# The first store and the fourth load in one queue: combining two expert outputs per token

## The chip, the cores and the metric

The kernel runs on one core of a Trainium2 chip. The metric is the device time in microseconds (us), the median over several executions. The core has five engines with instruction queues of their own; this kernel computes on VectorE (DVE in the profile) and a little on ScalarE (ACT), and moves data with the core's 16 DMA engines. Transfers are issued from two queues: that of SyncE (SP in the profile, DMA queue q1) and that of ScalarE (DMA queue q10).

## The reference

For each of 16 x 1024 tokens there are two expert outputs of 512 floats and two weights; the result is their weighted sum.

```python
def setup_inputs():
    batch, seq, hidden, n_experts, k = 16, 1024, 512, 8, 2
    return {
        "expert_outputs": np.random.randn(batch, seq, k, hidden).astype(np.float32),
        "combine_weights": np.random.randn(batch, seq, k).astype(np.float32),
    }

def reference(expert_outputs, combine_weights):
    weights = combine_weights[..., np.newaxis]
    return np.sum(expert_outputs * weights, axis=2).astype(np.float32)
```

67.1 MB of expert outputs are read and 33.6 MB of results are written, all in 32-bit floats.

## The kernel before

The 16,384 tokens are laid over 128 partitions, 128 tokens in each. A token's column holds both expert outputs, 1024 floats (4 KB), so a column over all partitions is 512 KB to load and 256 KB to store. The 128 columns are cut into ten tiles of 13 or 12 columns (`TILES`). In SBUF there is one buffer `et` with four rooms (`ROOM`), in which the tiles go round: tile g lies in room g mod 4. Tile 0 is loaded in two pieces of 2 and 11 columns, so that there are eleven loads (L76, the helper `load`), all of them issued from SyncE's queue. The weights come in three small transfers from ScalarE's queue (L79 and L114), behind an 8 KB store of zeros into a part of the output that is written again later (L111).

The order is written out by hand (`manual_schedule`); waits follow from the data and from a small set of completion semaphores that the transfers share in turn. First come the loads of tiles 0 to 3, in four rooms (`FIRST`). Then a loop runs over the stores (`STORES`): a round combines its tile, issues the store of the result, and issues the load of the tile four further on. That load goes into the room that the store reads from, so it waits for the store to have landed.

How a tile is combined (`combine`): for tiles 0 to 7 VectorE multiplies the whole room in place by the broadcast weights (L88) and adds the two halves into the beginning of the room (L97). Tile 8 is shared between ScalarE (L92) and VectorE (L94, L96, L97). Tile 9 goes column by column, ScalarE scaling one half (L102) and VectorE doing the other and the addition in one instruction (L103). Tiles 7 and 8 are stored together, and tile 9's result goes to room 0.

Stores are issued at L130: rounds 0 to 6 from ScalarE's queue, the joint store of tiles 7 and 8 and that of tile 9 from SyncE's. So before the change SyncE's queue holds: the loads of tiles 0, 1, 2, 3, then 4 to 9, each behind its wait, then two stores. ScalarE's queue holds the zeros, the weights, seven stores, and ScalarE's computing for tiles 8 and 9.

Of the kernel before, what the change touches and what calls it, by code (L numbers as in the profile page):

```python
# [1 line left out]

# [4 lines left out]


@with_exitstack
def kernel(  # L10
    ctx: ExitStack,
    tc: tile.TileContext,
    expert_outputs: bass.AP,
    combine_weights: bass.AP,
    out: bass.AP,
):

    nc = tc.nc
    b, s, k, h = expert_outputs.shape
    assert k == 2
    n = b * s
    P = nc.NUM_PARTITIONS
    per = n // P
    assert per * P == n

    ROOM = [13, 13, 12, 13]
    ROOMS = len(ROOM)  # L30
    SITE = [sum(ROOM[:i]) for i in range(ROOMS)]
    TILES = [13, 13, 12, 13, 13, 13, 12, 13, 13, 13]
    FIRST = [2, 11, 13, 12, 13]
    STORES = [[0], [1], [2], [3], [4], [5], [6], [7, 8], [9]]
    WHOLE = [0, 1, 2, 3, 4, 5, 6, 7]
    MIXED = [8]
    ALONE = 3
    FREE = {9: 0}
    LAST = 13
    assert all(c <= ROOM[g % ROOMS] for g, c in enumerate(TILES))  # L40
    assert sum(TILES) == per and [g for st in STORES for g in st] == list(range(len(TILES)))
    main = per - LAST
    starts = [sum(TILES[:g]) for g in range(len(TILES))]

    def rows(x):

        first = x[0 : P * main, :].rearrange("(p t) f -> p t f", p=P)
        second = x[P * main : n, :].rearrange("(p t) f -> p t f", p=P)
        return lambda t, c: first[:, t : t + c, :] if t < main else second[:, t - main : t - main + c, :]

    flat = out.rearrange("b s h -> (b s) h")
    eo = rows(expert_outputs.rearrange("b s k h -> (b s) (k h)"))
    cw = rows(combine_weights.rearrange("b s k -> (b s) k"))
    o = rows(flat)

    dt = mybir.dt.float32
    mult = mybir.AluOpType.mult
    add = mybir.AluOpType.add
    copy = mybir.ActivationFunctionType.Copy

    pool = ctx.enter_context(tc.tile_pool(name="all", bufs=1))
    et = pool.tile([P, sum(ROOM), k * h], dt)
    halves = et.rearrange("p j (k h) -> p (j k) h", k=k)
    wt = pool.tile([P, per * k], dt)
    wk = wt.rearrange("p (t k) -> p t k", k=k)
    zt = pool.tile([16, 128], dt)
    warm = pool.tile([P, 1], dt)

    def place(t):
        g = max(g for g in range(len(TILES)) if starts[g] <= t)  # L70
        return SITE[g % ROOMS] + t - starts[g]

    def load(t, c, **kw):
        at = place(t)
        assert place(t + c - 1) == at + c - 1
        nc.sync.dma_start(out=et[:, at : at + c], in_=eo(t, c), **kw)  # L76

    def weights(q, t, c):
        q.dma_start(out=wk[:, t : t + c, :], in_=cw(t, c))  # L79

    def combine(g, base):
        at, c, t0 = SITE[g % ROOMS], TILES[g], starts[g]
        if g in WHOLE or g in MIXED:
            room = halves[:, k * at : k * (at + c), :]
            x0, x1 = et[:, at : at + c, 0:h], et[:, at : at + c, h : 2 * h]
            if g in WHOLE:
                wb = wt[:, k * t0 : k * (t0 + c)].unsqueeze(2).to_broadcast([P, k * c, h])
                nc.vector.tensor_tensor(out=room, in0=room, in1=wb, op=mult)  # L88
            else:
                for i in range(ALONE, c):  # L90
                    x = et[:, at + i, 0:h]
                    nc.scalar.activation(out=x, in_=x, func=copy, scale=wt[:, k * (t0 + i) : k * (t0 + i) + 1])  # L92
                w1 = wk[:, t0 : t0 + c, 1:2].to_broadcast([P, c, h])
                nc.vector.tensor_tensor(out=x1, in0=x1, in1=w1, op=mult)  # L94
                w0 = wk[:, t0 : t0 + ALONE, 0:1].to_broadcast([P, ALONE, h])
                nc.vector.tensor_tensor(out=x0[:, 0:ALONE], in0=x0[:, 0:ALONE], in1=w0, op=mult)  # L96
            nc.vector.tensor_tensor(out=halves[:, base : base + c, :], in0=x0, in1=x1, op=add)  # L97
            return
        for i in range(c):
            t = k * (t0 + i)  # L100
            x0, x1 = halves[:, k * (at + i), :], halves[:, k * (at + i) + 1, :]
            nc.scalar.activation(out=x0, in_=x0, func=copy, scale=wt[:, t : t + 1])  # L102
            nc.vector.scalar_tensor_tensor(  # L103
                out=halves[:, base + i, :], in0=x1, scalar=wt[:, t + 1 : t + 2], in1=x0, op0=mult, op1=add
            )

    with tc.manual_schedule():
        nc.vector.memset(zt, 0.0)  # L108

        ahead = flat[0 : P * main, :].rearrange("(q t) h -> q (t h)", q=16)  # L110
        nc.scalar.dma_start(out=ahead[:, 0:128], in_=zt)  # L111
        weights(nc.scalar, 0, main)
        for half in (slice(0, P // 2), slice(P // 2, P)):
            nc.scalar.dma_start(out=wk[half, main:per, :], in_=cw(main, per - main)[half])  # L114
        nc.scalar.activation(out=warm, in_=nc.const_aps.tensor(1.0, (P, 1), dt), func=copy)  # L115

        t = 0
        for i, c in enumerate(FIRST):
            load(t, c, **({"max_dma_last_dim": k * h * 4} if i == 0 else {}))
            t += c  # L120
        assert t == sum(TILES[:ROOMS])
        for j, st in enumerate(STORES):
            room = FREE.get(st[0], st[0] % ROOMS)
            base, c = SITE[room] * k, 0
            for g in st:
                combine(g, base + c)
                c += TILES[g]
            assert c <= k * ROOM[room]
            q = nc.sync if j in (7, 8) else nc.scalar
            q.dma_start(out=o(starts[st[0]], c), in_=halves[:, base : base + c, :])  # L130
            for g in st:
                if g + ROOMS < len(TILES):
                    load(starts[g + ROOMS], TILES[g + ROOMS])


# [1 line left out]
_INS = ['expert_outputs', 'combine_weights']  # L137
_OUTS = [((16, 1024, 512), 'float32')]


# [23 lines left out]
```

## Time and profile before

| | |
|---|---|
| median of 3 runs | 238.98 us (238.86 to 240.7) |
| profiled execution, first to last instruction | 237.1 us |
| moved | 100.80 MB, 425 GB/s over the span |
| VectorE busy | 190.0 us |
| ScalarE busy | 15.8 us |

The span of the profiled execution is shorter than the times of the runs, which include what lies around the first and the last instruction. In the profile's rows a name such as `DVE L88` is the engine and the line of the kernel; `et<-et,wt` names what is written and read; `ACTq` and `SPq` are the instruction queues of ScalarE and SyncE, where a transfer is issued; `[1.10 <-DMA ...]` is the idle time ahead of an instruction and what ended it. A DMA engine's work is counted in packets: one packet here is one partition's part of a transfer, and each transfer ends on each engine with a small packet that reports its completion.

### The profile page before, as it was taken

The page shows a single profiled execution, that of the slowest core. Times are in us where ns is not written, and L with a number is a line of the kernel's source. Part 1 is how long each engine was busy: PE and PEld are TensorE (multiplying, and loading weights), DVE is VectorE, ACT ScalarE, POOL GpSimd, SP SyncE. Part 2 cuts the span into 40 slices and gives each one's busy share as a digit, 9 for nine tenths or more (in the row PEclk, how much of TensorE's full clock was granted, in tenths as well). Part 3 has the DMA queues.
Part 4 walks back from the last instruction along what each step waited for, and adds up shares of the span by engine and source line. Part 5 has one row for each costly group of instructions (what it writes and reads, how often), then busy time and mean ns, then how long its engine had stood idle before and what let it go on. Part 6 is the DMA issues. An engine that isn't in the chain of part 4 may idle for free.

```text
span 237.1 us, 154 instructions
## 1 busy us (share of the span) xinstructions
DVE 190.0 (80%) x33; ACT 15.8 (7%) x25; POOL 0.2 (0%) x4
## 2 busy tenths in 40 slices
DVE  0006999999999999999999998998499969919400
ACT  2000000000000000000000000000000055019200
POOL 0000000000000000000000000000000000000000
DMA  8999999989999999999899999999899999899996
GB/s 300 388 481 434 432 421 398 470 348 485 449 431 458 431 440 390 486 420 420 359 492 409 409 509 392 431 503 431 359 431 503 420 397 483 381 431 431 431 431 287
DMA packets 3344, 100.80 MB, mean 425 GB/s; under 512 B 512, under 2 KB 656, under 8 KB 912
## 3 DMA queue, kind: packets, MB, share of 16 engines
q1 hardware_dynamic: 2000, 77.33, 75.9%
q10 hardware_dynamic: 1344, 23.47, 23.0%
HBM read 67.24 MB, written 33.56 MB: 425 GB/s over the span
## 4 chain that ended last, share of the span: by engine, by line
DVE 55%; DMA 36%; issue 1%; ACT 0%; DVEq 0%; ACTq 0%; SPq 0%
DVE et L88 35%; DVE et L97 17%; DMA out_dram<-et 17%; DMA et<-in_expert_outputs_dram 12%; DMA wt<-in_combine_weights_dram 8%; DVE et L103 3%; ACT et L102 0%; DVEq L159 0%; ACTq L111 0%; DVE zt L108 0%; DVEq L88 0%; SPq L76 0%; ACTq L102 0%
## 5 line engine op out<-in xcount | busy, mean ns | idle before, releaser
L88 DVE TENSOR_TENSOR et<-et,wt 128x13312 f32<-128x13312 f32 (+1 forms) x8 | 110.0, 13754 | 23.8 <-DMA wt<-in_combine_weights_dram 18.7
L97 DVE TENSOR_TENSOR et<-et 128x6656 f32<-128x6656 f32 (+1 forms) x9 | 62.8, 6973 | 0.4
L92 ACT ACTIVATE et<-et,wt 128x512 f32<-128x512 f32 x10 | 6.2, 708 | 188.0 <-DMA et<-in_expert_outputs_dram 188.0
L103 DVE SCALAR_TENSOR_TENSOR et<-et,wt 128x512 f32<-128x512 f32 x13 | 8.7, 747 | 5.0 <-ACT et L102 5.0
L102 ACT ACTIVATE et<-et,wt 128x512 f32<-128x512 f32 x13 | 8.1, 707 | 14.0 <-DMA et<-in_expert_outputs_dram 14.0
L94 DVE TENSOR_TENSOR et<-et,wt 128x6656 f32<-128x6656 f32 x1 | 7.1, 7093 | 2.3 <-DMA et<-in_expert_outputs_dram 2.3
L96 DVE TENSOR_TENSOR et<-et,wt 128x1536 f32<-128x1536 f32 x1 | 1.8, 1751 | 0.0
L115 ACT ACT_TABLE_LOAD x1 | 1.3, 1283 | 3.1 <-issue 3.1
L108 DVE MEMSET zt<- 16x128 f32 x1 | 0.2, 165 | 0.8 <-PEq L148 0.8
L115 ACT ACTIVATE warm<-const-float32-1.0 128x1 f32<-128x1 f32 x1 | 0.2, 203 | 0.0
L148 POOL MEMSET const-bfloat16-1.0<- 128x1 bf16 x1 | 0.1, 102 | 0.0
L148 POOL MEMSET const-uint8-127<- 128x1 uint8 x1 | 0.1, 101 | 0.0
L148 POOL MEMSET const-float32-0.0<- 128x1 f32 x1 | 0.1, 99 | 0.2 <-issue 0.2
L148 POOL MEMSET const-float32-1.0<- 128x1 f32 x1 | 0.1, 98 | 0.0
## 6 DMA issues: line engine op xcount, KB each, us to landing
et<-in_expert_outputs_dram SPq DMA_DIRECT2D x7, 6656.0 KB, 32.2
out_dram<-et ACTq DMA_DIRECT2D x5, 3328.0 KB, 34.7
et<-in_expert_outputs_dram SPq DMA_DIRECT2D x2, 6144.0 KB, 41.1
out_dram<-et SPq DMA_DIRECT2D x1, 6656.0 KB, 19.9
out_dram<-et ACTq DMA_DIRECT2D x2, 3072.0 KB, 37.2
et<-in_expert_outputs_dram SPq DMA_DIRECT2D x1, 5632.0 KB, 18.2
out_dram<-et SPq DMA_DIRECT2D x1, 3328.0 KB, 14.0
et<-in_expert_outputs_dram SPq DMA_DIRECT2D x1, 1024.0 KB, 5.0
```

The costliest lines, as they stand in the source:

```text
L88: nc.vector.tensor_tensor(out=room, in0=room, in1=wb, op=mult)
L92: nc.scalar.activation(out=x, in_=x, func=copy, scale=wt[:, k * (t0 + i) : k * (t0 + i) + 1])
L94: nc.vector.tensor_tensor(out=x1, in0=x1, in1=w1, op=mult)
L96: nc.vector.tensor_tensor(out=x0[:, 0:ALONE], in0=x0[:, 0:ALONE], in1=w0, op=mult)
L97: nc.vector.tensor_tensor(out=halves[:, base : base + c, :], in0=x0, in1=x1, op=add)
L102: nc.scalar.activation(out=x0, in_=x0, func=copy, scale=wt[:, t : t + 1])
L103: nc.vector.scalar_tensor_tensor(out=halves[:, base + i, :], in0=x1, scalar=wt[:, t + 1 : t + 2], in1=x0, op0=mult, op1=add)
L108: nc.vector.memset(zt, 0.0)
L115: nc.scalar.activation(out=warm, in_=nc.const_aps.tensor(1.0, (P, 1), dt), func=copy)
L148: nc = _bacc.Bacc("TRN2", target_bir_lowering=False, num_devices=1)
```

## The change

The fourth load (tile 3) is taken out of the loads ahead of the loop. The first store (tile 0) is issued from SyncE's queue instead of ScalarE's, and right behind it in that queue the load of tile 3 (`BEHIND`), ahead of the load of tile 4. Sizes, rooms, the computing and all other transfers are as they were. SyncE's queue then holds the loads of tiles 0, 1, 2, the store of tile 0, the loads of tiles 3, 4 to 9, and two stores; ScalarE's queue starts its stores with that of tile 1.

```diff
-    FIRST = [2, 11, 13, 12, 13]
+    FIRST = [2, 11, 13, 12]
+    BEHIND = {0: [3]}
...
-        assert t == sum(TILES[:ROOMS])
+        assert t == sum(TILES[: ROOMS - 1])
...
-            q = nc.sync if j in (7, 8) else nc.scalar
+            q = nc.sync if j in (0, 7, 8) else nc.scalar
             q.dma_start(out=o(starts[st[0]], c), in_=halves[:, base : base + c, :])
+            for g in BEHIND.get(j, []):
+                load(starts[g], TILES[g])
             for g in st:
                 if g + ROOMS < len(TILES):
                     load(starts[g + ROOMS], TILES[g + ROOMS])
```

## The prediction

> **What bounds the kernel now.** I read the page first, for what is busy and how much is moved; then the busy time by stretches, for the rate of the DMA engines; then the timeline of VectorE and of the two DMA queues with the landing times, for who waits for whom. Names: L0 to L9 are the loads of tiles 0 to 9 (L0 in two pieces), S0 to S6 the stores of tiles 0 to 6, S78 the joint store of tiles 7 and 8, S9 the last.
>
> ```profile
> span 237.1 us, 154 instructions
> ...
> DVE 190.0 (80%) x33; ACT 15.8 (7%) x25; POOL 0.2 (0%) x4
> ...
> DMA packets 3344, 100.80 MB, mean 425 GB/s; under 512 B 512, under 2 KB 656, under 8 KB 912
> ...
> q1 hardware_dynamic: 2000, 77.33, 75.9%
> q10 hardware_dynamic: 1344, 23.47, 23.0%
> ```
>
> Queue q1 is SyncE's (all loads and two stores: 77 MB), q10 is ScalarE's. Their packets fill 75.9 + 23.0 = 98.9% of the 16 DMA engines' time; VectorE has 20% to spare. The stretches give the rate (columns: stretch, length, busy DVE, ACT, POOL, clock, DMA share, GB/s):
>
> ```profile
> 0.00:1.80 1.80, 0.17 (x1) 0.00 (x0) 0.20 (x4) 1.00 0.00 0
> 20.00:41.00 21.00, 20.96 (x3) 0.00 (x0) 0.00 (x0) 1.00 1.01 434
> 212.00:227.70 15.70, 8.71 (x13) 8.07 (x13) 0.00 (x0) 1.00 1.00 434
> 236.10:237.20 1.10, 0.00 (x0) 0.00 (x0) 0.00 (x0) 1.00 0.00 0
> ```
>
> The second row is loads alone, the third almost wholly the store S78: 434 GB/s both ways, so reading or writing makes no difference to the rate. 100.80 MB at 434 GB/s are 232.3 us; the empty 1.8 us ahead and about 1.0 us behind make 235.1. Of the span of 237.1 us only 2.0 us are lost while the engines run. The kernel is bound by its bytes, and the time changes only if the change makes the DMA engines stand still, or takes some of those 2.0 us away.
>
> Next, what sets the order. VectorE's tiles 3 to 8 begin, and stores S78 and S9 are issued, at:
>
> ```profile
> 81.32 14.02 DVE L88 TENSOR_TENSOR et<-et,wt 128x13312 f32<-128x13312 f32 x1
> 102.38 14.02 DVE L88 TENSOR_TENSOR et<-et,wt 128x13312 f32<-128x13312 f32 x1
> 123.44 14.02 DVE L88 TENSOR_TENSOR et<-et,wt 128x13312 f32<-128x13312 f32 x1
> 145.69 12.96 DVE L88 TENSOR_TENSOR et<-et,wt 128x12288 f32<-128x12288 f32 x1 [1.10 <-DMA et<-in_expert_outputs_dram]
> 169.18 14.03 DVE L88 TENSOR_TENSOR et<-et,wt 128x13312 f32<-128x13312 f32 x1 [3.94 <-DMA et<-in_expert_outputs_dram]
> 192.63 7.09 DVE L94 TENSOR_TENSOR et<-et,wt 128x6656 f32<-128x6656 f32 x1 [2.30 <-DMA et<-in_expert_outputs_dram]
> 208.61 0.35 SPq L130 DMA_DIRECT2D out_dram<-et  x1
> 222.29 0.34 SPq L130 DMA_DIRECT2D out_dram<-et  x1
> ```
>
> Up to tile 5 VectorE waits for no load, from tile 6 it waits for each: loads come at the pace of the DMA engines. The end, from the DMA issues (last column: us from issue to landing) of S78 and S9:
>
> ```profile
> out_dram<-et SPq DMA_DIRECT2D x1, 6656.0 KB, 19.9
> out_dram<-et SPq DMA_DIRECT2D x1, 3328.0 KB, 14.0
> ```
>
> S78 lands at 208.6 + 19.9 = 228.5, S9 at 222.3 + 14.0 = 236.3. They are 7.8 us apart, and S9's 3328 KB (3.41 MB) take 3.41 / 0.434 = 7.85 us: S9, issued 6.2 us before S78 landed, follows it in the queue without a gap. VectorE's waits therefore cost nothing as long as S78 and S9 are queued in time.
>
> **The change part by part.** *The store S0 moves to SyncE's queue, L3 behind it.* Before, L3 was issued at 4.92 and S0 at 40.91, and they landed 71.7 and 26.8 us later; S1 was issued at 61.97 and landed 29.4 us later:
>
> ```profile
> 4.92 0.33 SPq L76 DMA_DIRECT2D et<-in_expert_outputs_dram  x1
> 40.91 0.34 ACTq L130 DMA_DIRECT2D out_dram<-et  x1
> 61.97 0.34 ACTq L130 DMA_DIRECT2D out_dram<-et  x1
> ...
> et<-in_expert_outputs_dram SPq DMA_DIRECT2D x1, 6656.0 KB, 71.7
> ...
> out_dram<-et ACTq DMA_DIRECT2D x1, 3328.0 KB, 26.8
> ...
> out_dram<-et ACTq DMA_DIRECT2D x1, 3328.0 KB, 29.4
> ```
>
> So S0 landed at 67.7, L3 at 76.6, S1 at 91.4. How the two queues shared the engines is seen in the packets by queue, in four windows (to 45.0; 45.7 to 46.1; 46.1 to 64.1, two rows; 69.0 to 69.5):
>
> ```profile
> q1 hardware_dynamic: 656, 18.35, 96.9%
> ...
> q10 hardware_dynamic: 16, 0.43, 246.8%
> ...
> q1 hardware_dynamic: 112, 4.98, 64.1%
> q10 hardware_dynamic: 96, 2.56, 32.9%
> ...
> q10 hardware_dynamic: 16, 0.43, 197.4%
> ```
>
> S0's first packets, one on each engine, start at 45.75 (mid-window), 4.8 us after its issue. In the next 18 us the engines take 96 store packets and 112 on the load queue, 16 of which are the small ones that close L2: one for one. A load packet is 53,248 B (6656 KB over 128), a store packet 26,624 B; at 434 / 16 = 27.1 GB/s a pair takes 1.97 + 0.98 = 2.95 us. S1 starts at about 69.2.
>
> After the change: S0's issue is still released by the same addition, at 40.9. Ahead of it in its queue is the rest of L2. L0 to L2 are 38 rows of 512 KB, 19.9 MB; 18.35 MB had started by 45.0, in packets that end where S0's began, so the other 1.6 MB take 1.6 / 0.434 = 3.6 us more: L2 is out at 45.75 + 3.6 = 49.4 instead of 53. S0 then runs alone, 3.41 / 0.434 = 7.9 us, to 57.2; it starts later and lands 10 us earlier. L3, issued at about 41.3, starts at 57.2. Both are queued 8 us before their turn: that is the cover under which the late issue of L3 costs nothing. Without it the engines would stand until the issue.
>
> *ScalarE's queue begins with S1.* Issued at 62.0 as before; with the 4.8 us that S0 needed, it starts at 66.8, and the alternation begins there. L3 has had 9.6 us alone by then, 4.2 of its 6.8 MB; the other 2.6 MB alternate two to one with S1, 2.6 x 1.5 / 0.434 = 9.0 us: L3's data are in at 75.8, and landed, with a store's turn ahead of the closing packet, by about 77.3. VectorE wants it at 81.32. Slack 4.0 us, and no wait.
>
> *All that is queued behind.* SyncE's queue is passed by S0 alone; behind S0 stand L3 and L4 to L9. Before, L4 was issued at 67.7, when S0 had landed; now it may go at about 57.6, with L3 still ahead of it until 76. That wait disappears without a gain, because L3 ends last. Stores begin 69.2 - 66.8 = 2.4 us sooner, which is 2.4 / 2.95 = 0.8 of a store packet per engine, or 0.8 us of work taken from the loads. I take 0.8 us as the lag of all later loads; the bounds are 0 and, if S1 joined 1.1 us after its issue (below), (2.4 + 3.7) / 2.95 x 0.98 = 2.0 us. ScalarE's queue must not run dry for this to hold, and it doesn't: S1 is issued at 62.0, S6 at 165.3, while the store ahead of each is in flight (S5 until 183.9):
>
> ```profile
> 165.27 0.34 ACTq L130 DMA_DIRECT2D out_dram<-et  x1
> ...
> 144.62 39.25 DMA out_dram<-et
> ...
> 183.92 28.80 DMA et<-in_expert_outputs_dram
> ```
>
> The last two are from the chain of waits: S5 lands, L9 goes out, and lands at 212.7. L4, issued at 67.80, landed 32.2 us later at 100.0, and L5, issued at 91.42, landed 31.8 us later:
>
> ```profile
> 67.80 0.33 SPq L76 DMA_DIRECT2D et<-in_expert_outputs_dram  x1
> 91.42 0.33 SPq L76 DMA_DIRECT2D et<-in_expert_outputs_dram  x1
> ...
> et<-in_expert_outputs_dram SPq DMA_DIRECT2D x1, 6656.0 KB, 32.2
> ...
> et<-in_expert_outputs_dram SPq DMA_DIRECT2D x1, 6656.0 KB, 31.8
> ```
>
> With the lag they land at 100.8 (wanted at 102.4) and 124.0 (wanted at 123.4: VectorE waits 0.6 us, for the first time at tile 5). Tiles 6 to 8, which wait already, begin 0.8 us later, and S78 is issued at 209.4. L9's landing stays at 212.7: everything that the engines move ahead of its end, ten loads and S0 to S6, is the same. So S9's issue stays at 222.3, 5.8 us before its turn.
>
> *The cover of S78.* From issue to first packet a queue needs 1.1 us where nothing is ahead (the first load of all):
>
> ```profile
> 0.73 183.52 SPq L76 DMA_DIRECT2D et<-in_expert_outputs_dram  x11
> ```
>
> (0.73 to the end of the empty stretch, 1.8.) S78 must be out by 212.7 - 1.1 = 211.6; it is out at 208.6 now, 209.4 after. Of 3.0 us of slack 2.2 remain, and even the lag of 2.0 us fits. Were a store's start to take longer than a load's, up to the 212.7 - 208.6 = 4.1 us that S78 had here, the lag would show at the end: +0.8 us, with the bound for the lag +2.0. I take 0, since S78 and S9 stand next to the loads of one queue.
>
> *A load behind a store in one queue* stands nowhere in this trace. The nearest row is S9 behind S78, a gap of 0; the farthest a write with its confirmation and nothing to speak of in it, the 8 KB store ahead of all:
>
> ```profile
> out_dram<-zt ACTq DMA_DIRECT2D x1, 8.0 KB, 3.9
> ```
>
> If L3 could start only when S0's writes are confirmed, up to 3.9 us would be lost; a gain is excluded, since L3 can't start before S0's packets are out. I take 0, after the row nearest in kind and size. The Trainium skill, "DMA: Bandwidth & Descriptors", section on the anatomy of one DMA, speaks for the other side: it gives a transfer a fixed cost of about 2.0 us, most of it the receipt of the last write, HBM being the heaviest target. Paid between S0 and L3 it would make the time 241.0, an estimate; S9's 7.8 us behind S78 doesn't show it paid between two stores.
>
> Sum: 0 (S0) + 0 (L3 late) + 0 (lag) + 0 (queue) = 0. The span stays 237.1 us; the median of the three runs, 238.98, is 1.9 us above it, so 239.0.
>
> **The rivals.** *Slower: the queue stands still between S0 and L3.* At 57.2 ScalarE's queue is empty until S1 comes at 66.8, so a halt there has no cover, and in a kernel bound by bytes it goes through to the end. Up to 3.9 us: 239.0 to 242.9. It decides, past 1%, from 2.4 us on. For it: no such order in the trace; against: S9 behind S78, and loads on loads at 434 GB/s. *Slightly slower: S78 comes late*, by 0.3 to 2.0 us, if loads lag more or a store's start takes longer: 239.3 to 241.0; against it the 2.2 us of slack. *Slightly faster:* some of the 2.0 us that are lost under way belong to S0's meeting with L2 and vanish: 237.0 at the very best, 238.5 if a quarter does. That is at most 0.8%. *The change moves nothing:* if engines took turns by whole transfers, S0 would follow L2 in both versions; the one-for-one packets speak against it, and the time would be 239.0 as well.
>
> **How the numbers follow.** No change 0.72, S78 late 0.10, a small gain 0.08, the halt 0.08 (0.06 of it above 2.4 us), nothing moved 0.02. One per cent is 2.4 us, about what a measurement tells here from no change, as the three runs lie between 238.86 and 240.7. Slower by over 1%: the 0.06 of the halt. Faster: the cap of 0.8% leaves 0.02, for its being read from one execution. Same: 0.92. The forecast's own range is 238.5 to 239.5; I reach down to 238.3 for the small gain and up to 240.2 for half of the late S78 and of a short halt, which leaves out some 2 in 10.
>
> **What would show it.** Right: S0 lands near 57.6 and L3 near 77; L4 is issued ten us earlier and lands near 101; a new short wait of VectorE at tile 5; S78 issued near 209.4; L9 and S9 land where they did; both queues' shares still add up to 99%. Wrong: a stretch between 49 and 67 with a DMA share clearly under 1; L3 landing past 81.3; S78's issue past 211.6, with an empty stretch before 213; L9 landing elsewhere than near 212.7.

## The result and the profile after

| | before | after |
|---|---|---|
| median of 6 runs each | 238.9 us | 240.38 us (239.69 to 241.59) |
| ratio, with its 95% interval | | 1.0063 (1.0041 to 1.0085) |
| span of the profiled execution | 237.1 us | 237.9 us (run of 239.69), again 238.4 (run of 240.23) |

The change makes the kernel slower by 0.6%, 1.5 us. That is little, but the interval of the ratio leaves 1 out, and 240.38 us lies above the range that was given (238.3 to 240.2). The first profile after fell on the fastest of its runs (239.69 us); a second one of the same kernel, taken with the experiments (240.23 us), stands nearer to the median and is used for the sizes.

The page after:

```profile
span 237.9 us, 154 instructions
...
DVE 190.2 (80%) x33; ACT 15.8 (7%) x25; POOL 0.2 (0%) x4
...
q1 hardware_dynamic: 2144, 80.74, 79.2%
q10 hardware_dynamic: 1200, 20.06, 19.6%
```

3.4 MB have gone from q10 to q1, and the two shares still add up to 98.8%: by the page the DMA engines are as full as before. A packet that takes longer counts as busy for longer, so this share can't show a lengthened packet. Either packets have become longer, or the engines end less evenly. The timeline has the order that was forecast, with larger shifts:

```profile
40.66 0.35 SPq L131 DMA_DIRECT2D out_dram<-et  x1
...
58.75 0.33 SPq L77 DMA_DIRECT2D et<-in_expert_outputs_dram  x1
...
102.70 14.03 DVE L89 TENSOR_TENSOR et<-et,wt 128x13312 f32<-128x13312 f32 x1 [0.49 <-DMA et<-in_expert_outputs_dram]
...
126.04 14.03 DVE L89 TENSOR_TENSOR et<-et,wt 128x13312 f32<-128x13312 f32 x1 [2.18 <-DMA et<-in_expert_outputs_dram]
...
211.18 0.34 SPq L131 DMA_DIRECT2D out_dram<-et  x1
```

L4 goes out at 58.75, when S0 has landed; VectorE waits at tile 4 already, and 2.2 us at tile 5; S78 is issued at 211.18. The chain of waits shows L9's landing:

```profile
147.22 33.46 DMA out_dram<-et
...
180.73 32.77 DMA et<-in_expert_outputs_dram
```

(The second row begins at L9's issue; 180.73 + 32.77 is its landing.) L9 lands at 213.5 instead of 212.7, and all that follows is as much later.

**Where the time is.** In a window of one microsecond in which each of the 16 engines starts one packet, the share of the queue is the mean time of a packet in hundredths of a us. Before the change, the packets by queue in three such windows (41.5 to 42.5; 43 to 44, the load packets just ahead of S0's first; 210 to 211, those just ahead of S78):

```profile
q1 hardware_dynamic: 16, 0.79, 182.1%
...
q1 hardware_dynamic: 16, 0.79, 220.2%
...
q1 hardware_dynamic: 16, 0.85, 196.6%
```

A packet of tile 2's load, 49,152 B, takes 1.82 us; the one ahead of the first store takes 2.20. At 210 us, ahead of S78, a packet of 53,248 B takes the 1.97 us that it takes anywhere. After the change, the packets ahead of S0's first (46.5 to 47.5), and in the second profile (46.8 to 47.8):

```profile
q1 hardware_dynamic: 16, 0.79, 291.8%
```

```profile
q1 hardware_dynamic: 16, 0.79, 246.3%
```

2.92 and 2.46 us: 1.10 and 0.65 us are lost by each engine on average at the turn from L2 to S0, where the kernel before lost 0.4 in all. A second loss shows in the window from 63 to 72 us, in which S1 joins (loads' queue; before, and the second profile after):

```profile
q1 hardware_dynamic: 48, 2.56, 65.5%
```

```profile
q1 hardware_dynamic: 55, 2.93, 81.1%
```

65.5% of 9 us on 16 engines over 48 packets is 1.97 us for one, the usual time; 81.1% over 55 packets is 2.12 us: (2.12 - 1.97) x 55 / 16 = 0.5 us lost. In the first profile after, this second loss is 0.2 us. In both profiles of the changed kernel no packet after 72 us is longer than usual by more than some hundredths.

The engines do not lose alike. The packets that start from 235 us on (before; second profile after):

```profile
q1 hardware_dynamic: 16, 0.00, 0.4%
```

```profile
q1 hardware_dynamic: 33, 0.45, 42.3%
```

Before, only the 16 small closing packets are left; after, 17 large packets of S9 still start there: one for each engine and one more. The last data packet ends at 235.77 us on the mean of the engines and at 235.98 on the slowest before, at 236.58 and 237.26 in the second profile after. The spread arises at the same two turns. The 16 small packets that close a transfer, one on each engine, show it: before, they start within 0.32 us of each other for every transfer from L2 to S9. In the second profile after it is 0.40 us for L1, 0.87 for L2, ahead of S0, 2.1 for L3, behind the place where S1 joins, and 1.03 for S9. (In the first profile after it is 0.46, 0.41, 0.63 and 0.63: the sizes differ from one execution to the next.)

### The profile page after: what moved, and what is told of

Same layout as the page of the kernel before. It is cut to its first block, busy times and chain, and to the rows that moved or that the text cites. A ratio compares the mean times of both kernels' runs of the same rounds, so it can differ in the third digit from the quotient of the medians.

```text
span 237.9 us, 154 instructions
## 1 busy us (share of the span) xinstructions
DVE 190.2 (80%) x33; ACT 15.8 (7%) x25; POOL 0.2 (0%) x4
## 4 chain that ended last, share of the span: by engine, by line
DMA 62%; DVE 30%; ACT 0%; DVEq 0%; issue 0%; ACTq 0%; SPq 0%
DMA et<-in_expert_outputs_dram 30%; DMA out_dram<-et 25%; DVE et L89 18%; DVE et L98 9%; DMA wt<-in_combine_weights_dram 8%; DVE et L104 3%; ACT et L103 0%; DVEq L162 0%; ACTq L112 0%; DVE zt L109 0%; DVEq L89 0%; SPq L77 0%; ACTq L103 0%
```

## The experiments

The losses below are worked out from the packets of each trace: the time of load packets (and of stores' where they are lengthened) above the usual one of their size (1.665, 1.815, 1.966 us; 0.987 and 0.912 for stores), summed and divided by 16. One profiled execution stands for each kernel, so a loss is known to some tenths of a us. "First" is the loss at the first start of large stores, "later" all behind it up to 125 us. Ratios are to the kernel before on the same chip. The diffs of e2, f3, g3, h1 and h2 are against the kernel before, the others against the changed one.

| kernel | time, us | ratio (95%) | first | later |
|---|---|---|---|---|
| before | 238.9 | 1 | 0.43 | 0 |
| changed | 240.4 | 1.0063 (1.0041 to 1.0085) | 1.10 | 0.21 |
| e1, changed again | 240.16 | 1.0055 (1.0040 to 1.0070) | 0.65 | 0.57 |
| e2, store alone | 242.89 | 1.0170 (1.0155 to 1.0185) | 0.48 | 1.56 |
| e3, load late alone | 238.87 | 1.0006 (0.9996 to 1.0015) | 0.53 | 0 |
| e4, small store first | 240.18 | 1.0053 (1.0036 to 1.0070) | 0.70 | 0.64 |
| f1, VectorE quiet | 241.16 | 1.0096 (1.0076 to 1.0116) | 0.84 | 1.29 |
| f2, wide store first | 240.91 | 1.0097 (1.0064 to 1.0130) | 0.08, then 0.54 | 0.14 |
| f3, VectorE busy at the end | 238.84 | 1.0000 (0.9991 to 1.0010) | 0.38 | 0.18 |
| f4, two stores | 244.47 | 1.0236 (1.0220 to 1.0251) | 0.71 | 0.95 |
| g1, load behind the turn held | 240.74 | 1.0084 (1.0067 to 1.0101) | 0.56 | 0.96 |
| g2, load on ScalarE's queue | 241.84 | 1.0138 (1.0097 to 1.0178) | 0.20 | 0.61 |
| g3, load behind the end | 243.94 | 1.0214 (1.0193 to 1.0234) | 0.41 | 0 |
| h1, second store held | 241.58 | 1.0115 (1.0098 to 1.0132) | 0.35 | 0.96 |
| h2, small packets at the end | 238.89 | 1.0001 (0.9992 to 1.0010) | 0.40 | 0 |
| h3, store alone, then both | 240.31 | 1.0065 (1.0051 to 1.0079) | 0.38 | 1.08 |

**The change in parts.** First the same kernel again, then each half of the change alone.

> The changed kernel once more, for a second profile. Theory A (the first store of the run makes the engines halt when it stands in the loads' own queue): the last packets of tile 2's load take about 2.9 us instead of 1.8 again, a loss of about 1.1 us at 47 to 50 us, and the time is about 240.4. Theory B (the loss at that place is chance, and the time varies for another reason): the loss at 47 to 50 differs by more than 0.5 us, with the time.

The losses are at the same two places, and their sum (1.22 us here, 1.31 in the first profile) is steadier than either. The first loss differs by 0.45 us between the two profiles, just under what theory B asked for, and not with the time: the execution with the larger loss is the faster one by 0.5 us (239.69 against 240.23). Its engines ended more evenly: the slowest was 0.3 us behind the mean there, 0.7 here. So the places are no chance, and the sizes vary.

```diff
-            q = nc.sync if j in (7, 8) else nc.scalar
+            q = nc.sync if j in (0, 7, 8) else nc.scalar
```

> The first store goes to SyncE's queue, but behind the load of tile 3, which is issued early as in the kernel before. Theory A (first store in the loads' own queue): a loss of about 1.1 us at the turn from the load of tile 3 to the store, near 65 us, and about 240.2. Theory C (the late issue of the load of tile 3, or its place behind a store, costs the time): no such loss, 238.9.

Neither number was met. The turn from L3 to S0 loses 0.48 us, but the time rises by 4 us, for another reason that I had not seen: S0, behind L3, lands only near 81.8 us, L4 waits for it in the same room, and until then no load is queued. S1, from ScalarE's queue, shares the engines with S0, so that stores run alone from 65 to 80.6 us. From 80.6 to 82 us the DMA engines stand still:

```profile
80.60:82.00 1.40, 1.40 (x2) 0.00 (x0) 0.00 (x0) 1.00 0.01 0
```

When the loads come back beside the stores, 1.5 us more are lost in long packets (84 to 90 us). Later S78 goes out only at 215.0, and the engines stand still for another 0.9 us ahead of it. So this half cannot be judged alone; what it gives is a second place, behind stores that ran alone.

```diff
-            q = nc.sync if j in (0, 7, 8) else nc.scalar
+            q = nc.sync if j in (7, 8) else nc.scalar
...
             for g in BEHIND.get(j, []):
+                nc.vector.memset(et[:, SITE[3] : SITE[3] + 1, 0:1], 0.0)
                 load(starts[g], TILES[g])
```

> The first store stays in ScalarE's queue; the load of tile 3 alone is made late: it waits for a one-column write of VectorE into its room, behind the first addition, so that it is issued near 41 us. Theory A: as the kernel before, 238.9 to 239.2, with the 0.4 us that the engines lost there when the first store came. Theory C (late load): about 240.4.

```profile
41.03 0.37 ACTq L131 DMA_DIRECT2D out_dram<-et  x1
41.05 0.33 SPq L77 DMA_DIRECT2D et<-in_expert_outputs_dram  x1
```

L3 is issued at 41.05, as in the changed kernel, and the median is that of the kernel before to 0.06% (238.87 us; single runs go up to 239.79, and the profile is of that one). The late issue costs nothing, as forecast; theory C falls.

**Is it that a first store is slow?** Two kernels write something earlier from the loads' own queue.

```diff
+            if i == 3:
+                nc.sync.dma_start(out=ahead[:, 128:256], in_=zt)
             load(t, c, **({"max_dma_last_dim": k * h * 4} if i == 0 else {}))
```

> The changed kernel with an 8 KB store of zeros in SyncE's queue between the loads of tiles 1 and 2 (into a part of the output that the first store writes again). Theory A1 (the first store in a queue pays, whatever its size): the loss moves to about 34.5 us and the turn to the first large store near 49 us loses nothing; 240.4 or, if a small store pays less, 239.3. Theory A2 (only a large store behind a long stretch of loads pays): the loss of 1.1 us stays near 49 us, 240.5.

0.70 us are lost near 47 us, none near 34.5: a small store ahead takes nothing off.

```diff
+    wide = pool.tile([P, h], dt)
...
+        nc.vector.memset(wide, 0.0)
...
+            if i == 2:
+                nc.sync.dma_start(out=o(0, 1), in_=wide.unsqueeze(1))
             load(t, c, **({"max_dma_last_dim": k * h * 4} if i == 0 else {}))
```

> The changed kernel with a 256 KB store of zeros from all 128 partitions in SyncE's queue between the loads of tiles 0 and 1 (into rows that the first store writes again); its bytes alone are 0.6 us. Theory A (the first store of all partitions pays, once): the loss moves to about 19 us, none near 49 us; about 240.8 in all. Theory E (each time that stores start while the engines have only loads, they lose time): a loss at 19 and at 49 and at 65 us; 241.0 to 241.6.

Inconclusive: 0.08 us near 17 us, 0.54 near 48 us, 0.14 later, and runs from 240.06 to 241.76, the profile being of the lowest. In that one execution the wide store neither takes the loss over nor adds one like it.

**Is it VectorE, reading and writing SBUF at the same time?** It is busy at the turn to S0 and idle at the turn to S78, which loses nothing. One kernel makes it idle at the first, another busy at the second.

```diff
+    quiet = pool.tile([P, 1], dt)
...
+            if g == 1:
+                nc.vector.tensor_copy(out=quiet, in_=et[:, SITE[2], 0:1])
```

> The changed kernel, but VectorE waits for the load of tile 2 before it multiplies tile 1 (a copy of one column, that only serves to wait), so that it stands still from 41 to 50 us, over the turn from that load to the first store. Theory D (VectorE's use of SBUF is what makes the engines halt at that turn, as it stands still at the later turn to the store of tiles 7 and 8, where no loss is): the mean packet ahead of the store takes 1.8 to 1.9 us, no loss near 49 us. Theory A (a first large store behind a stretch of loads): 0.65 to 1.1 us lost as before. The time says little: VectorE is about 10 us late, of which it can make up some 7.

```diff
+            if j == 7:
+                spare = halves[:, k * SITE[2] : k * SITE[2] + 7, :]
+                nc.vector.tensor_tensor(out=spare, in0=spare, in1=spare, op=mult)
```

> The kernel before, with a multiplication on VectorE that nothing needs (3584 columns of a room that is out of use, about 3.8 us), behind tile 8's addition, so that VectorE is busy at the turn from the last load to the store of tiles 7 and 8 near 212 us. Theory D (VectorE's use of SBUF): 0.5 to 1.1 us lost at 210 to 213 us, the time 239.5 to 240. Theory A: nothing lost there, 238.9.

With VectorE quiet, from 41 to 50.7 us, the turn to S0 still loses 0.84 us (packets from 46.8 to 47.8):

```profile
q1 hardware_dynamic: 16, 0.79, 265.6%
```

With VectorE busy from 208.65 to 212.5, packets ahead of S78 (210 to 211 us) are as short as ever:

```profile
208.65 3.88 DVE L133 TENSOR_TENSOR et<-et 128x3584 f32<-128x3584 f32 x1
```

```profile
q1 hardware_dynamic: 16, 0.85, 196.6%
```

Theory D falls on both sides.

**Is it what stands behind the store, or the queue?**

```diff
-    BEHIND = {0: [3]}
+    BEHIND = {}
...
                 nc.vector.tensor_tensor(out=room, in0=room, in1=wb, op=mult)
+                if g == 1:
+                    nc.vector.memset(et[:, SITE[3] : SITE[3] + 1, 0:1], 0.0)
+                    load(starts[3], TILES[3])
+                    load(starts[4], TILES[4])
...
-                if g + ROOMS < len(TILES):
+                if 0 < g < len(TILES) - ROOMS:
```

> The changed kernel, but the load of tile 3 (and that of tile 4 behind it) is held back until VectorE has multiplied tile 1, near 54.5 us: the turn from the load of tile 2 to the first store, near 49 us, then has nothing queued behind the store, as the turn to the store of tiles 7 and 8 at 212 us has not. The store runs alone until 57, so that the later issue has 2.5 us of cover. Theory F (the engines lose the time because a load stands behind the store): no loss near 49 us, and 239.3 to 239.6. Theory A (stores that start after a long stretch of loads): 0.65 to 1.1 us lost near 49 us, 240.2.

The packets ahead of S0's first (46.8 to 47.8):

```profile
q1 hardware_dynamic: 16, 0.79, 237.7%
```

With nothing behind S0 the turn still loses 0.56 us, and 0.96 follow. Theory F falls.

```diff
             for g in BEHIND.get(j, []):
-                load(starts[g], TILES[g])
+                nc.vector.memset(et[:, SITE[3] : SITE[3] + 1, 0:1], 0.0)
+                nc.scalar.dma_start(out=et[:, SITE[3] : SITE[3] + 13], in_=eo(starts[g], 13))
```

> The changed kernel, but the load of tile 3 goes, also at 41 us, to ScalarE's queue ahead of the second store, so that it joins the load of tile 2, and the turn to the first store in SyncE's queue, near 57 us, comes while ScalarE's queue holds loads. Theory E (stores that start while the engines have nothing but loads cost 0.2 to 1.1 us, whichever queue): a loss near 57, none where the second load stream joins near 45, about 240. Theory G (any queue that starts again after it was empty costs about 0.4): 0.4 us lost near 45 us, none near 57, 239 to 239.5.

A load that joins loads near 45 us loses nothing, which speaks against theory G: the restart of a queue is not enough. S0, beginning near 57 us beside a load, loses 0.20. The time is worse for the reason of e2 (L4 is issued late) and for one of the rivals: S78 is issued at 213.68, and the engines stand still for 2.0 us on average ahead of it. So these 241.84 us say nothing on the losses.

```diff
+            if j == 7:
+                nc.sync.dma_start(out=et[:, SITE[2] : SITE[2] + 4], in_=eo(0, 4))
```

> The kernel before with a load that nothing needs (4 columns, 2.1 MB, 4.8 us of bytes) in SyncE's queue behind the store of tiles 7 and 8, ahead of the last store. Theory F: 0.5 to 1.1 us lost at the turn to that store near 212 us; 244.2 to 244.8. Theory A: nothing lost there, 243.7.

243.94 us, with no long packet at 212 us nor at 227 us, where the added load follows S78 alone. A load behind a store is not enough to make a loss.

**Does each start of stores cost, and does their packet size matter?**

```diff
-    BEHIND = {0: [3]}
+    BEHIND = {0: [3], 1: [4]}
...
-            q = nc.sync if j in (0, 7, 8) else nc.scalar
+            q = nc.sync if j in (0, 1, 7, 8) else nc.scalar
...
-                if g + ROOMS < len(TILES):
+                if 0 < g < len(TILES) - ROOMS:
```

> The changed kernel with the second store too in SyncE's queue, between the loads of tiles 3 and 4 (so SyncE's queue holds loads 0, 1, 2, store 0, load 3, store 1, loads 4 and on); ScalarE's queue begins with the store of tile 2, near 81 us. Theory A (once only): a loss of 0.65 to 1.1 us near 49 us, none at the turn near 73 us from the load of tile 3 to the second store, and 0.2 to 0.6 us where ScalarE's queue joins near 85 us. Theory E (every time stores start beside nothing but loads): 0.5 us or more at 73 us too, and the time 0.5 us or more above the changed kernel's.

The turn from L3 to S1 loses 0.34 us, by each theory too little or too much, and smaller losses follow at the start of each later store (0.1 to 0.4 us each, up to 186 us). Stores have run alone here from 49.5 to 57 us and from 74 to 80 us. The time is mostly something else: the loads lag so far that S78 is issued at 217.07, and the engines stand still for 3.3 us on average.

```profile
217.07 10.41 SPq L131 DMA_DIRECT2D out_dram<-et  x2
```

```diff
-    STORES = [[0], [1], [2], [3], [4], [5], [6], [7, 8], [9]]
+    STORES = [[0], [1], [2], [3], [4], [5], [6], [7], [8], [9]]
...
-    FREE = {9: 0}
+    FREE = {9: 2}
...
-            q = nc.sync if j in (7, 8) else nc.scalar
+            q = nc.sync if j in (7, 8, 9) else nc.scalar
```

> The kernel before with the joint store of tiles 7 and 8 cut into two stores, so that the store behind the last load near 212 us has packets of 26,624 B as the first store has, not 53,248 (tile 9's result then goes to the room of tile 6). Theory H (small store packets behind load packets make the loss): 0.5 us or more lost near 212, 239.4 to 240. Theory E or A without it: none there, 238.9.

Nothing is lost at 212 us, and the time is unchanged: small store packets behind load packets are not enough to make a loss, and theory H falls. Whether S0's turn would lose less with large packets was not tried.

```diff
-                nc.vector.tensor_tensor(out=room, in0=room, in1=wb, op=mult)
+                if g == 2:
+                    nc.vector.tensor_tensor(out=room[:, 0:16], in0=room[:, 0:16], in1=wb[:, 0:16], op=mult)
+                    nc.vector.memset(quiet, 0.0)
+                    nc.scalar.activation(out=warm, in_=quiet, func=copy)
+                    nc.scalar.dma_start(out=o(starts[1], TILES[1]), in_=halves[:, SITE[1] * k : SITE[1] * k + TILES[1], :])
+                    load(starts[5], TILES[5])
+                    nc.vector.tensor_tensor(out=room[:, 16:], in0=room[:, 16:], in1=wb[:, 16:], op=mult)
+                else:
+                    nc.vector.tensor_tensor(out=room, in0=room, in1=wb, op=mult)
...
+            if j == 1:
+                continue
```

> The kernel before, with the second store held back to about 70.5 us (tile 2's multiplication is cut in two parts of 16 and 8 half columns, and the store waits for the first part), so that after the first store has ended near 65.5 the engines have loads alone for some 9 us before stores start again. Theory E (each new start of stores beside nothing but loads costs 0.2 to 0.6 us): a second loss of 0.2 to 0.6 us near 72 to 78 us, besides the 0.4 at 43 to 48. Theory A (only the first start costs): none there. The time rises with the loss and with what the held store delays: 239.2 to 240.5 by E, 238.9 to 239.5 by A.

This run turned the question round. Its packets in four windows: 72.8 to 73.8, ahead of the second start of stores (16 of the 32 are small closing packets); 96.2 to 101.5, two rows; 101.9 to 102.9:

```profile
q1 hardware_dynamic: 32, 0.85, 197.5%
...
q10 hardware_dynamic: 112, 2.36, 107.0%
q1 hardware_dynamic: 16, 0.00, 0.2%
...
q1 hardware_dynamic: 16, 0.85, 254.7%
```

After some 9.5 us of loads alone the stores start again at 74.9, and no packet is longer: theory E falls as a rule for every new start of stores. But holding S1 makes L5 late, so that from 96 to 102 us stores run alone, and where the loads come back a packet takes 2.55 us instead of 1.97; 0.96 us are lost there in all. In e2 it was the same, and in the changed kernel S0 runs alone from 50 to 57 us ahead of its second loss. f1 has it too: behind S0 alone, 0.4 us are lost where S1 joins (76 to 80 us); stores run alone again from 97 to 103 us, and 0.3 us are lost where the loads come back and 0.5 where the stores rejoin them (114 to 118 us). The last kernel puts such a stretch into the kernel before, without S0 in the loads' queue:

```diff
-    BEHIND = {0: [3]}
+    BEHIND = {}
...
+                if g == 1:
+                    nc.vector.memset(et[:, SITE[3] : SITE[3] + 1, 0:1], 0.0)
+                    load(starts[3], TILES[3])
+                    load(starts[4], TILES[4])
...
-            q = nc.sync if j in (0, 7, 8) else nc.scalar
+            q = nc.sync if j in (7, 8) else nc.scalar
...
-                if g + ROOMS < len(TILES):
+                if 0 < g < len(TILES) - ROOMS:
```

> The first store stays in ScalarE's queue, as before the change; the load of tile 3 (and that of tile 4 behind it) is held back to 54.5 us, so that the first store, which joins the load of tile 2 at 45.7, has its last packets alone from 53 to 57 us, then the load of tile 3 is alone, and the second store joins near 66. Theory J (after a stretch of stores alone the engines lose time once loads and stores meet again): 0.3 to 0.5 us near 43 to 48 as before the change, and 0.2 to 0.6 us between 57 and 72 us as in the changed kernel; 239.2 to 239.7. Theory K (all of the loss comes from the first store standing behind loads in their own queue): nothing lost from 57 to 72, 238.9.

Two windows, 53.2 to 57 and 57 to 69 us:

```profile
q10 hardware_dynamic: 64, 1.70, 103.9%
...
q1 hardware_dynamic: 87, 4.63, 98.1%
```

From 53.2 to 57 only S0's packets start. Then 87 load packets take 98.1% of 12 us on 16 engines, 2.17 us each instead of 1.97: (2.165 - 1.966) x 87 / 16 = 1.08 us. The first start loses 0.38 as in the kernel before, and the time, 240.31 us, is that of the changed kernel. Theory K falls: with S0 in ScalarE's queue, where its start loses 0.4 us, the stretch of stores alone is followed by losses all the same. Theory J has the place right, but not the size: it allowed 0.2 to 0.6 us and at most 239.7. g1, which holds L3 back in the same way with S0 in SyncE's queue, loses 0.96 there, so the queue of S0 makes little of this second loss. Why it is 1 us in these two and 0.2 to 0.6 in the changed kernel, where L3 is queued long before its turn, is open.

## Why the prediction was wrong

The step that failed is the sum, "0 (S0) + 0 (L3 late) + 0 (lag) + 0 (queue) = 0", in its first term. I let S0 run alone between L2 and L3 at no cost, on the ground that loads alone and stores alone both go at 434 GB/s, "so reading or writing makes no difference to the rate". That is true inside each stretch; what costs here is to go from the one to the other and back to both. In the second profile after, 0.65 us go at the turn to S0 and 0.57 where S1 later joins the loads; 0.43 us of the kernel before, where S0 joined L2, go away. That is 0.8 us on the mean of the engines (235.77 to 236.58). The other 0.5 us are unevenness, which grows at these two turns: the slowest engine was 0.2 us behind the mean and is 0.7 behind now, and the slowest ends the kernel. 0.8 + 0.5 = 1.3 us, against 1.3 measured for that kernel in its own comparison (238.86 to 240.16). The sum of the prediction worked with the DMA engines as one pipe of 434 GB/s and had no term for either. Its sign of being wrong, a DMA share under 1 between 49 and 67 us, could not show it: the share there is 1.03.

The row that could have warned was in the profile before: the load packets ahead of S0's first take 2.20 us, not 1.82. Of the 2.0 us "lost while the engines run" I thought only of what the change might win back, not that the turn to S0, made within one queue, could cost more. The rival of a small gain did have a true part: 0.43 of the 2.0 us belonged to S0's meeting with L2 and went away.

Point by point:

- *The order of the queues*: right. S0 runs behind L2 and alone, and lands at 58.7 us (57.6 forecast); L3 begins at 57.7 and S1 at 65.6 (66.8).
- *L3 late costs nothing*: right, shown by e3 alone.
- *A load behind a store in one queue costs nothing*: right. After the change, L3's first packets start from 57.65 us on, before S0 has landed at 58.7, so L3 didn't wait for that landing. The Trainium skill ("DMA: Bandwidth & Descriptors", "Anatomy of one DMA") gives about 2.0 us as the fixed cost of a transfer issued from GpSimd, and the prediction carried the figure over to SyncE's queue. By this trace no such time is paid between S0 and L3. So the rival's halt between S0 and L3 did not come: what is lost at S0 lies in the load packets ahead of the store, not behind it.
- *The lag of the loads*, 0.8 us with bounds of 0 and 2.0: too small. L8 lands at 195.1 instead of 192.5, so 2.6 us. S1 begins 3.5 us sooner than before (65.6 against 69.1), not 2.4, which by the prediction's rule is 3.5 / 2.95 x 0.98 = 1.2 us, an estimate; the losses add 1.10 + 0.21 - 0.43 = 0.9; the remaining 0.5 us are open. VectorE's new waits are 0.5 and 2.2 us, not 0 and 0.6.
- *S78's cover*: it held. S78 goes out at 211.18, and on each engine its first packet follows L9's last at once. The prediction wanted it out by 211.6, 1.1 us ahead of L9's landing. As that landing moved to 213.5, 1.2 us of the slack of 3.0 were left; in the second profile S78 goes out at 211.69, past 211.6, and costs nothing either, with L9 landing at 214.0. In e2, g2 and f4, which lag more, the rival "S78 late" came true.
- *L9's landing stays*: wrong by 0.8 us, in the second profile by 1.3: the losses and the unevenness.

What stays open is why these turns lengthen a packet. Shown is where it happens: at the first start of large stores, and at the return to loads and stores together after stores alone. Shown is also that VectorE is not needed for it (f1), nor the load behind the store (g1), and that a busy VectorE (f3), small store packets (h2), a load behind a store (g3) or a pause of the stores (h1) do not make it by themselves. It isn't explained why L9 to S78 is free, why the first turn costs from 0.5 to 1.1 us in kernels alike there, why f4 goes on losing a little at each later store, nor where the 0.18 us of f3 near 91 us come from, which follow no stretch of stores alone.

No version here beats the kernel before.

## What to carry to other kernels

Where the DMA engines bound a kernel, count not only bytes and empty stretches, but look at the time of single packets where a stream of the other direction starts: a window in which each engine starts one packet gives it from the queue's share. Loads and stores that alternate from two queues ran here at full rate, in h1 also after a pause of the stores; a stretch of stores alone was followed by losses of 0.1 to 1.6 us when both came together again. And a time that ends with the slowest of 16 engines grows with their spread, which no mean share shows.

## What the runs showed of the hardware that was not expected

A packet of 53,248 B took 1.966 us as a load and as a store (S78), and a store packet of 26,624 B 0.987 us, alone or alternating with loads, except at a few turns, where a load packet took up to 3.18 us instead of 1.815 (changed kernel, 47 us). A load from a second queue that joined the loads of the first cost nothing (g2, 0.03 us in all of tile 2's packets); loads that join stores after a stretch of stores alone cost 1.0 us in h1 and 1.5 in e2. The 16 engines, which kept within 0.32 us of each other before the change, came apart by up to 2.1 us at these turns and ended 1.03 us apart (second profile after).
